# Five edits to a tuned hard-max attention kernel: the last four tiles compared whole, the first segment's rows as words, larger loads, gathers two a tile, key units later

## The chip, the cores and the metric

The kernel runs on one core of a Trainium2 chip. The metric is the device time of one execution in microseconds (us), as the median of the fast executions of a kernel. The kernel before takes 438.6 us. Every run of another kernel was made on one chip together with runs of the kernel before. A ratio is the mean time of one kernel's fast runs over that of the other's of the same rounds, so it is not quite the ratio of the medians that I quote; an interval is a 95% interval.

PE is TensorE, DVE is VectorE, ACT is ScalarE, POOL is GpSimd and SP is SyncE. A profile was taken of one execution of each kernel. All times within an execution are microseconds from the start of its span; "L310" is a line of the kernel that the profile is of, and line numbers differ a little from kernel to kernel.

## The reference

```python
# q, k, v: (4, 4096, 128) fp32, normal draws
logits = np.matmul(q, k.transpose(0, 2, 1))
best = np.argmax(logits, axis=-1)
return v[b_idx, best, :].astype(np.float32)
```

For each of 4 x 4096 queries the key with the greatest product is sought, and its row of v is the result. That is 128 tiles of 128 queries.

## The kernel before

For each tile, PE makes products in fp16 (`pd`, `psn`), ACT turns them into codes (`A`, `E`), and DVE folds them into words (`W`) and takes the eight greatest (`TOP`, a MAX8). The low bits of the best word name a group of keys (`cand`). POOL gathers those keys in fp16 (`kg`), DVE multiplies them with the queries (`prod`, `p1`, `p2`, `D`) and picks, and POOL gathers the rows of v (`vr`), which SP stores. Rows where fp16 can't decide are "flagged": their indices are compacted with one-hot matrices on PE, at tile 64 for the first half (a "segment") and after the last tile for the second, their keys and queries are gathered in fp32 (`FK`, `FQ`), compared, and their rows of v (`FV`) scattered over what was stored (`out`). Two more tiles, the last ones, are compared whole in fp32 (`gather_whole`, `dots_whole`, `pick_whole`), so that their candidates need no flags.

POOL issues all gathers and many loads, in the order in which this function hands them out once per tile:

```python
def issue(it):
    n = 0
    ...
    while near_q and (n < 1 + behind or near_q[0] in marks or it >= T - 1):   # kg: one a tile
        g = near_q.pop(0)
        n += g not in marks
        g()
    ...                                                                       # then vr, at a rate
```

```python
def gathers(t):
    ...
        m = 4 if t1 <= 116 else 2
        if t0 <= t < t1 and t < T - 2 and (t - t0) % m == m - 1:
            gather(c, t - m + 1, m)      # four kg come due at once
```

The loads of the next batches' keys and queries go out on the same POOL queue in 8-row pieces:

```python
        elif 10 <= qt < 18 and qt % 2 == 0:
            load_part(b + 1, qt - 2)
        elif 18 <= qt < 26 and qt % 2 == 0:
            load_part(b + 2, qt - 18)
```

The end of the program, after the last TOP, is: flags of the second segment up to the word index `row`, gathers of FK and FQ, exact comparison, FV, and then

```python
        get(FV, v_flat, win, B * Sk)
        nc.gpsimd.indirect_dma_start(out=out_flat, out_offset=IOA(ap=rowk, axis=0), in_=FV, ...)   # "out"
```

after which every engine runs its closing instructions.

## Time and profile before

| what | before |
|---|---|
| median time | 438.6 us |
| span of the profiled execution | 436.54 us |
| first TOP / last TOP (tile 127) start | 19.4 / 408.28 us |
| last TOP to the issue of `out` | 24.07 us |
| issue of `out` to the end of the span | 4.19 us |

The last three rows add up to the span (408.28 + 24.07 + 4.19): the loop, the tail, the end. How ACT, DVE and POOL share these stages is read in the prediction below. The view of groups: line, engine, operation, out <- in, shapes, count | busy us, mean ns of one | idle time of the engine before them, and what ended it.

```profile
L311 DVE TENSOR_TENSOR prod<-kg,natq 128x768 f16<-128x768 f16 x63 | 34.4, 546 | 0.2 <-DMA kg<-k,cand 0.2
...
L927 POOLq DRAIN  x3: 46/109/3253, 432.1 to 436.3; - x3
```

DVE waits 0.2 us in all for gathered keys. POOL's sequencer has three DRAINs in the closing code, the longest of 3.253 us, starting at 432.1, with the issue of `out`.

### The profile page before, as it was taken

To read this page: it belongs to the slowest core of one execution; us is meant where nothing else is said; L and a number is where in the kernel's file an instruction comes from. 1 tells how busy PE (TensorE), PEld (TensorE's weight loads), DVE (VectorE), ACT (ScalarE), POOL (GpSimd) and SP (SyncE) were. 2 spreads that over 40 slices of the span, in tenths; PEclk is the share of its full clock that TensorE was granted. 3 is DMA by queue.
4 is the path that set the end of the run, shared out by engine and by line. 5 is a ranking of instruction groups with operands and counts; after the bars stand their busy time and mean duration, and the time that the engine had idled before them with its cause. 6 is when DMAs were issued, how large, how long until landed. Compare 5 with 4: busy or idle time off the path is not lost.

```text
span 436.5 us, 6165 instructions
## 1 busy us (share of the span) xinstructions
PE 377.1 (86%) x1830; PEld 167.7 (38%) x1830; DVE 406.6 (93%) x722; ACT 378.2 (87%) x446; POOL 304.3 (70%) x335
## 2 busy tenths in 40 slices
PE   7999999999999999999999888989889988885010
PEld 4444444444444444444444433433333333332000
DVE  2788999999999999999999999999999999999961
ACT  4999999999999999999999888999999988985010
POOL 8423456777767786777778776777767677777773
PEclk9999999999999999999999999999999999999555
DMA  7943999473326999663336985452423232333441
GB/s 127 204 108 72 158 141 144 103 134 81 108 55 133 174 166 189 127 113 100 92 95 138 172 148 116 93 143 76 119 76 92 82 85 81 93 95 99 116 131 52
DMA packets 52868, 50.54 MB, mean 116 GB/s; under 512 B 34136, under 2 KB 40890, under 8 KB 52832
## 3 DMA queue, kind: packets, MB, share of 16 engines
q0 software_dynamic: 19072, 33.87, 39.7%
q1 hardware_dynamic: 33760, 16.26, 15.8%
q8 instruction: 14, 0.23, 0.2%
q14 instruction: 22, 0.18, 0.2%
HBM read 40.05 MB, written 14.55 MB: 125 GB/s over the span
## 4 chain that ended last, share of the span: by engine, by line
ACT 37%; issue 23%; DVE 16%; PE 9%; POOL 8%; DMA 6%; POOLq 0%; ACTq 0%; DVEq 0%; SPq 0%
ACT A L245 32%; DVE TOP L275 6%; ACT E L258 5%; DVE W L271 5%; POOL vr L353 4%; PE psn L228 3%; POOL kg L293 3%; PE pd L228 3%; PE psn L255 3%; DMA vr<-in_v_dram,win 2%; DMA natk<-in_k_dram 2%; DVE prod L311 1%; DVE p L316 1%; DMA vr<-in_v_dram,win_w 1%; DMA kg<-k,cand 1%
## 5 line engine op out<-in xcount | busy, mean ns | idle before, releaser
L245 ACT ACTIVATE A<-pd 128x1024 f16<-128x1024 f32 x253 | 257.0, 1043 | 10.8 <-PE pd L228 10.3
L293 POOL DMA_INDIRECT kg<-k,cand x126 | 124.5, 988 | 79.8 <-DVE cand L287 48.8
L271 DVE SCALAR_TENSOR_TENSOR W<-psn,E 128x1024 int16<-128x1024 f32 x128 | 166.4, 1300 | 6.8 <-PE psn L255 4.1
L228 PE MATMUL psn<-kT,qT 128*128 128x512 f16 x512 | 151.9, 378 | 16.2 <-ACT A L245 7.5
L228 PE MATMUL pd<-kT,qT 128*128 128x512 f16 x506 | 150.4, 379 | 6.6 <-ACT A L245 6.3
L275 DVE MAX8 TOP<-W 128x8 f32<-128x1024 f32 x128 | 156.0, 1219 | 0.0
L228 PEld LDWEIGHTS <-qT 128*128 128x128 f16 x1018 | 97.2, 97 | 153.0 <-issue 62.9
L353 POOL DMA_INDIRECT vr<-in_v_dram,win x126 | 125.9, 1000 | 39.5 <-issue 35.3
L255 PE MATMUL psn<-A,identh 128*128 128x512 f16 x512 | 152.0, 378 | 0.0
L258 ACT ACTIVATE E<-psn 128x1024 int16<-128x1024 f32 x128 | 132.3, 1033 | 4.6 <-PE psn L255 4.1
L255 PEld LDWEIGHTS <-identh 128*128 128x128 f16 x512 | 49.6, 97 | 60.8
L311 DVE TENSOR_TENSOR prod<-kg,natq 128x768 f16<-128x768 f16 x63 | 34.4, 546 | 0.2 <-DMA kg<-k,cand 0.2
L208 ACT ACTIVATE kT<-uk 128x256 f16<-128x256 f32 x48 | 20.4, 426 | 0.8 <-PE uk L205 0.8
L316 DVE TENSOR_TENSOR p<-prod 128x768 f16<-128x768 f16 (+1 forms) x34 | 17.7, 520 | 0.2
L321 DVE TENSOR_REDUCE D<-p 128x12 f32<-128x384 f16 (+1 forms) x34 | 17.2, 506 | 0.1
L204 PE MATMUL uk<-identh,natk 128*128 128x128 f16 x96 | 15.8, 218 | 0.0
L512 ACT ACTIVATE far_e<-iota_h,posn_e 128x128 f16<-128x128 f16 x2 | 0.8, 393 | 14.7 <-DVE posn_e L504 14.7
L495 PE MATMUL fp_e<-n_e,tri 128*128 128x1 f32 x2 | 0.6, 348 | 13.9 <-DVE n_e L493 13.9
L205 PEld LDWEIGHTS <-natk 128*128 128x128 f16 x96 | 9.3, 97 | 7.0 <-issue 4.5
L66 POOL DMA_DIRECT2D natk<-in_k_dram x19 | 11.3, 601 | 0.8 <-POOLq L916 0.8
L204 PEld LDWEIGHTS <-natk 128*128 128x128 f16 x96 | 9.4, 98 | 5.6
L319 DVE TENSOR_TENSOR p<-p 128x384 f16<-128x384 f16 (+1 forms) x34 | 11.3, 331 | 0.1
(158 smaller groups left out, 153.4 us busy)
## 6 DMA issues: line engine op xcount, KB each, us to landing
out_dram<-vr SPq DMA_DIRECT2D x31, 256.0 KB, 2.2
natq<-in_q_dram POOLq DMA_DIRECT2D x12, 256.0 KB, 5.3
natk<-in_k_dram POOLq DMA_DIRECT2D x10, 256.0 KB, 5.7
k<-kd SPq DMA_DIRECT2D x18, 128.0 KB, 3.4
k<-natk POOLq DMA_DIRECT2D x6, 384.0 KB
kg<-k,cand POOLq DMA_INDIRECT x126, 2.7
vr<-in_v_dram,win POOLq DMA_INDIRECT x126, 2.7
natk<-in_k_dram POOLq DMA_DIRECT2D x8, 128.0 KB, 6.5
```

What stands on the lines that cost most here:

```text
L204: nc.tensor.matmul(out=o, lhsT=natk[b % 2][:, h, 4 * m + x, :], rhs=identh, start=True, stop=False)
L208: nc.scalar.activation(out=kT[b % 2][:, c:c + 256], in_=ps, func=AF.Copy)
L228: nc.tensor.matmul(out=ps[:, n * 512:(n + 1) * 512], lhsT=qT[b % 2][:, qt * P:(qt + 1) * P], rhs=kT[b % 2][:, u * 1024 + n * 512:u * 1024 ...
L245: nc.scalar.activation(out=A, in_=ps, func=AF.Abs)
L255: nc.tensor.matmul(out=ps[:, n * 512:(n + 1) * 512], lhsT=identh, rhs=A[:, n * 512:(n + 1) * 512], start=False, stop=True)
L258: nc.scalar.activation(out=E, in_=ps, func=AF.Relu, scale=QSCALE)
L271: nc.vector.scalar_tensor_tensor(out=W_t[t % NW].bitcast(I16)[:, 1::2], in0=ps, scalar=QSCALE, in1=E, op0=OP.mult, op1=OP.max)
L275: nc.vector.max(out=TOP[:, t, :], in_=W_t[t % NW].bitcast(FP32))
L293: near_q.append(lambda j=j: nc.gpsimd.indirect_dma_start(out=kg[:, j].rearrange("p f d -> p (f d)"), out_offset=None, in_=k16[t0 // NQT], ...
L311: nc.vector.tensor_tensor(out=prod[:, i:i + h], in0=kg[:, i:i + h], in1=natq[b % 2][:, x + i - b * NQT:x + i + h - b * NQT, :].unsqueeze(2 ...
L316: nc.vector.tensor_tensor(out=p1, in0=prod[:, :, :, 0:64], in1=prod[:, :, :, 64:128], op=OP.add)
L353: late_q.append(lambda j=j: nc.gpsimd.indirect_dma_start(out=vr[:, j, :], out_offset=None, in_=v_flat, in_offset=IOA(ap=win[:, i + j:i + j ...
```

## The change

Its intent: (a) "whole": the last four tiles instead of two are compared whole in fp32, so their dots leave the tail; (b) "words": the first segment gets its keys' indices from words that are already there, as the second one does, rather than by fetching a record back; (c) "loads": 8-row pieces become 16-row pieces, at fewer tiles; (d) "gathers": two kg a tile instead of one from tile 4 to 111, so that dots start earlier; (e) "units": ACT's key units of the first batch three tiles later. Cut to its core:

```diff
-LATE = 4
+LATE = 2
+WHOLE = 4
...                                       # (b) in flag_segment, many small steps out, wider ones in
+        low_words(t0, S)
+        EC = ...tensor_tensor(CG * F)     # 4 x S at once, then four MAX8
-        nc.vector.tensor_copy(out=bs, in_=ps[:, 0:1])
+        nc.scalar.activation(out=bs, in_=ps[:, 0:1], func=AF.Copy)
-        get(FR, rec, rr, P * T)
+        gb, row = places(t0, ps2)
...                                       # (a)
-    cuts = list(range(0, 96 + 1, 8)) + list(range(96 + 4, T - 3, 4)) + [T - 2, T]
+    cuts = list(range(0, 96 + 1, 8)) + list(range(96 + 4, T - 7, 4)) + [T - 6, T - 4, T]
...                                       # (d)
-        while near_q and (n < 1 + behind or near_q[0] in marks or it >= T - 1):
+        while near_q and (n < (2 if 4 <= it < 112 else 1) + behind or near_q[0] in marks or it >= T - 1):
...                                       # (e)
-        units += [(x - 1, x - NQT + (6 + 3 * i // 2 if b == 1 else 1 + 2 * i), unit_k, b, i) for i in range(16)]
+        units += [(x - 1, x - NQT + (9 + 3 * i // 2 if b == 1 else 1 + 2 * i), unit_k, b, i) for i in range(16)]
...                                       # (c)
-        elif 10 <= qt < 18 and qt % 2 == 0:
-            load_part(b + 1, qt - 2)
-        elif 18 <= qt < 26 and qt % 2 == 0:
-            load_part(b + 2, qt - 18)
+        elif qt in (11, 19):
+            load_part(b + 1, 8 + (qt - 11) // 2, 16)
+        elif qt in (23, 27):
+            load_part(b + 2, qt - 23, 16)
```

## The prediction

> **What bounds the kernel now.** I read the page first (DVE busy 93%, ACT 87%, PE 86%, POOL 70% of 436.5 us), then the busy time by stretches, because a share averaged over the span hides stages with different limits. Columns: busy microseconds of PE, PEld, DVE, ACT and POOL in the stretch, then clock, DMA share, GB/s.
>
> ```profile
> 20.00:40.00 20.00, 19.13 (x98) 8.73 (x96) 16.77 (x17) 20.00 (x25) 5.24 (x6) 1.00 0.50 97
> 100.00:120.00 20.00, 19.64 (x96) 8.73 (x95) 20.00 (x31) 20.00 (x25) 14.23 (x16) 1.00 0.33 90
> ...
> 240.00:260.00 20.00, 17.50 (x91) 7.95 (x90) 19.94 (x45) 17.12 (x21) 15.47 (x17) 1.00 0.98 156
> ...
> 340.00:360.00 20.00, 17.81 (x76) 7.17 (x74) 19.83 (x31) 18.16 (x20) 14.15 (x15) 1.00 0.31 88
> ...
> 410.00:420.00 10.00, 1.36 (x8) 1.02 (x8) 8.19 (x52) 1.31 (x4) 7.61 (x8) 0.50 0.46 132
> 420.00:437.00 17.00, 0.59 (x2) 0.50 (x2) 5.24 (x40) 0.00 (x0) 7.96 (x8) 0.50 0.32 91
> ```
>
> There are three stages. Until about 240 us ACT is full, and DVE is full too from 60 us on; only before that has DVE slack (3.2 us in 20 to 40). From 240 us to about 409 us DVE alone is full and ACT waits. After the last TOP (408.28 us) comes a tail of 28 us with no large work. Next the groups, for the size of the steps, and the timeline, for what they really cost from start to start:
>
> ```profile
> L245 ACT ACTIVATE A<-pd 128x1024 f16<-128x1024 f32 x253 | 257.0, 1043 | 10.8 <-PE pd L228 10.3
> L293 POOL DMA_INDIRECT kg<-k,cand x126 | 124.5, 988 | 79.8 <-DVE cand L287 48.8
> L271 DVE SCALAR_TENSOR_TENSOR W<-psn,E 128x1024 int16<-128x1024 f32 x128 | 166.4, 1300 | 6.8 <-PE psn L255 4.1
> ```
>
> ```profile
> 102.51 1.22 DVE L275 MAX8 TOP<-W 128x8 f32<-128x1024 f32 x1
> 103.65 1.29 DVE L271 SCALAR_TENSOR_TENSOR W<-psn,E 128x1024 int16<-128x1024 f32 x1
> 104.82 0.55 DVE L311 TENSOR_TENSOR prod<-kg,natq 128x768 f16<-128x768 f16 x1
> 105.29 1.22 DVE L275 MAX8 TOP<-W 128x8 f32<-128x1024 f32 x1
> ```
>
> Start to start TOP takes 1.14, W 1.17 and prod 0.47 us: durations overlap, so a removed step gives back somewhat less than its duration. A tile needs W + TOP (2.31 to 2.34), a quarter of a four-tile dot group (two prod, 0.46, 0.26, 0.45: about 0.54) and a share of a pick: about 2.95 us on DVE, the pace until 208 us (TOP 0 to TOP 64: 188.6 us / 64). From there to TOP 127 it is 200.3 / 63 = 3.18 us, because the first segment's flags and the smaller picks are added on DVE.
>
> The tail, in order of time (start, duration):
>
> ```profile
> 408.28 1.23 DVE L275 MAX8 TOP<-W 128x8 f32<-128x1024 f32 x1
> ...
> 410.20 0.55 DVE L311 TENSOR_TENSOR prod<-kg,natq 128x768 f16<-128x768 f16 x1
> ...
> 411.94 0.95 POOL L580 DMA_INDIRECT xk<-in_k_dram,xc  x1 [0.30 <-DVE D L321]
> ...
> 413.19 1.10 POOL L353 DMA_INDIRECT vr<-in_v_dram,win  x1 [0.30 <-issue]
> ...
> 417.18 0.15 DVE L525 TENSOR_SCALAR row_e<-rs_e 128x1 uint32<-128x1 f32 x1
> ...
> 418.51 1.01 POOL L528 DMA_INDIRECT FK<-in_k_dram,gb_e  x1 [0.30 <-DVE XD L585]
> ...
> 426.44 1.02 POOL L353 DMA_INDIRECT vr<-in_v_dram,win_w  x1 [0.30 <-issue]
> 428.30 1.00 POOL L528 DMA_INDIRECT FV<-in_v_dram,xw_fe  x1 [0.84 <-DVE xw_fe L623]
> 432.35 1.02 POOL L557 DMA_INDIRECT out_dram<-FV,rowk_e  x1 [3.05 <-DMA out_dram<-vr]
> ```
>
> What is to be seen: POOL issues one gather every 1.3 us without a pause from 401 to 427 us (0.30 us between two that waits for nothing). The word index row_e is there at 417.33 us, yet FK starts 1.2 us later, behind four vr gathers. The last step waits for the store of the last vr pair (issued 426.44, landed 2.75 later, stored 2.09 later). So two chains run side by side in the tail, DVE to row_e and POOL's queue, and the queue is the later one.
>
> **What the Trainium skill says.** "Perfetto Trace Analysis", section "DMA Instruction — SWDGE (GPSIMD)": the profiled end of such a DMA is the end of descriptor generation, not of the data's movement. The trace agrees: a gather shows 0.95 to 1.0 us on POOL and lands 2.7 us after its issue (median in the DMA list), so a load twice as large need not cost POOL twice. "DMA: Bandwidth & Descriptors", section "Anatomy of one DMA — SWDGE (gpsimd) path": about 2.0 us fixed plus the bytes; the 2.7 us and the 5.3 to 5.7 us of the 256 KB loads fit in order. "VectorE: DVE Perf Modes", section "The TRN2 errata — SBUF-src ops pay a fixed extra latency per instruction": a small operation is mostly a fixed cost. Here operations on 1 to 12 elements take 0.13 to 0.23 us, so what counts in the flag code is their number. "ScalarE: Activation LUTs", section "What ACT_TABLE_LOAD costs": 186 ns + 0.833 ns per element, 93 ns overlap; for 1024 that is 1039 ns, and the trace has 1043.
>
> **The change part by part.**
>
> *Last four tiles whole.* The dots of tiles 124 and 125 leave the tail: from prod at 410.20 to the pick at 411.86, 1.66 us off DVE's chain to row_e. Picks keep their number (the last groups become 120-122 and 122-124, both done before TOP 127). One one-hot moves from ACT to DVE: DVE ends its four at 416.0, ACT its two at 416.64; with five and one both end near 416.1, 0.5 us less. Together row_e comes 2.2 us earlier, some 415.1. Eight further fp32 dot products at 0.21 us (417.29 to 419.00 for the present eight) add 1.7 us of DVE, but while FK and FQ are still coming. POOL gains nothing in count: 126 kg + 126 vr + 2 + 2 become 124 + 124 + 4 + 4, always 256 gathers. From 401.2 us to FV I count 20 of them before; written out in the new order (one xk, three vr, xk, two vr, xk, vr, xk, two vr, four FK/FQ, four vr of the whole tiles) it is 20 again. At 1.3 us each FK would start near 416.8, the last vr pair near 426.1 instead of 426.44 us. So of DVE's 2.2 us POOL lets through 0.3 to 1.6 us, the larger value if one vr that now runs at 398.49 is done before. Taken: 0.9.
>
> *First segment as words.* Removed on DVE, by the groups' durations: Ec 0.22, two sums 0.40, bs and tot 0.28, a cast 0.17, tp to row (seven) 1.01, rr twice 0.29, bo, gi, gb 0.50: 2.87 us. Added, from their twins in the last segment: CG 0.50, EC 0.43, three MAX8 0.47, two rec 0.35, gb, rs, row 0.46: 2.21 us. Net 0.66 us less, on a full DVE (240 to 320 us): taken as 0.5. ACT gets five small operations (an estimate of 1.5 us) in a stretch where it has 14% idle. POOL loses one gather (1.3 us) and a wait for it.
>
> *Loads.* 34 direct loads become 24 (8-row pairs merged); ten at 0.60 + 0.30 us free 9 us of POOL, but POOL sets nothing before the tail, and prod waits for kg only 0.2 us in the whole run. Value 0 directly.
>
> *Gathers two a tile.* The four kg of a group go out in two tiles rather than four, so its dots begin up to two tiles earlier. The number of operations stays. Its worth is at the start: two tiles' dots (2 x 0.54 us) move into DVE's slack before 60 us, out of the time in which DVE is full. Taken 0.6.
>
> *Key units three tiles later.* 16 of 48 ACT operations of 0.43 us move inside a stretch in which ACT is full before and after: 0.
>
> Sum: 0.9 + 0.5 + 0.6 = 2.0 us; 438.6 - 2.0 = 436.6, and I put 436.4 because a lighter POOL may start the tail less behind.
>
> **The rivals.** (1) *POOL's queue does not hold the tail*: if lighter loads leave POOL idle before 400 us, the whole 2.2 us of DVE, and the last pair with it, come through, and with DVE's gains in the loop the time is near 434. For it: POOL is 2 us behind DVE at xk (409.6 to 411.94), which ten fewer loads could remove. Against it: by then the vr of a pick start only about 3 us after it (win at 398.06, its first vr at 401.20), so the backlog of loads long past is already gone. (2) *The larger loads delay the kg behind them*, and DVE, which has no slack after 60 us, stands still: some 1 us for each of ten loads, 440 or more. For it: landings rise to 4 to 6 us beside loads. Against it: loads now go out at tiles 11, 19, 23, 27 of 32, and kg always at the two tiles before and again two tiles later, 5.9 us apart. (3) *Nothing but noise*: four vr of the whole tiles instead of two come after FK and end later than now, eating the gain: 438.5. (4) The ACT copies of bs and tot stand in ACT's queue, and posn waits there: up to 1 us worse.
>
> **Range and chances.** The parts spread from -5 to +2 us; 8 in 10 from 433.8 to 438.9. Faster by 2% would need 429.8 us, more than every gain I can name together; slower by 2% (447.4) would need rival 2 at four times its size.
>
> **What would show it.** The steps hold if TOP 127 starts 0.5 to 1.5 us earlier, if the stretch 20 to 60 us has more DVE work, if the way from TOP 127's start to row_e's end (408.28 to 417.33, 9.05 us) shrinks by about 2 us, and if POOL is still without pauses until the last vr pair. A wait of prod for kg above 1 us in total would make rival 2 right. POOL with pauses before FK would make rival 1 right. A TOP 127 that starts later than 408.3 would make the prediction wrong in the loop, where I expect almost nothing.

## The result, and the profile after

The changed kernel takes 443.68 us (443.13 to 443.88, 4 runs) against 438.53: ratio 1.0114, interval [1.0096, 1.0131]. It is 1.1% slower where 0.5% faster was predicted.

| | before | after | difference |
|---|---|---|---|
| last TOP | 408.28 | 411.28 | +3.00 |
| last TOP to `out` | 24.07 | 23.23 | -0.84 |
| `out` to the end of the span | 4.19 | 7.34 | +3.15 |
| span | 436.54 | 441.85 | +5.31 |

So the tail did what was predicted (0.9 us), and two losses stand against it: one in the loop, one after the last transfer was issued. The stretches first (PE, PEld, DVE, ACT, POOL busy; clock; DMA share; GB/s), of the changed kernel:

```profile
20.00:40.00 20.00, 19.44 (x93) 8.57 (x92) 17.82 (x18) 20.00 (x25) 5.23 (x6) 1.00 0.56 101
...
240.00:260.00 20.00, 17.90 (x94) 8.31 (x94) 19.90 (x42) 18.37 (x29) 13.71 (x14) 1.00 0.79 143
280.00:300.00 20.00, 17.78 (x87) 7.79 (x86) 19.03 (x44) 18.22 (x23) 13.47 (x14) 1.00 0.47 111
```

DVE has 1.05 us more work in 20 to 40 (17.82 against 16.77), as the prediction wanted. ACT is full in that stretch, and nothing comes of it: TOP of tile 20 starts 0.10 us earlier than before, TOP of tile 32 starts 0.2 us later. Between 280 and 300 us, where DVE was full before (19.97 us), it stands still for a microsecond. The groups of the changed kernel say what for:

```profile
L292 POOL DMA_INDIRECT kg<-k,cand x124 | 121.0, 976 | 90.2 <-DVE cand L286 59.5
...
L310 DVE TENSOR_TENSOR prod<-kg,natq 128x768 f16<-128x768 f16 x62 | 34.1, 550 | 2.8 <-DMA kg<-k,cand 2.8
```

The wait of prod for kg has grown from 0.2 to 2.8 us. POOL is less busy than before (67% against 70%), so it isn't overloaded on average. The timeline (start, duration, engine, line, operation, idle time before it) shows how the wait comes about, here for the first one:

```profile
145.14 0.95 POOL L352 DMA_INDIRECT vr<-in_v_dram,win  x1 [0.30 <-issue]
146.40 1.39 POOL L352 DMA_INDIRECT vr<-in_v_dram,win  x1 [0.30 <-issue]
147.79 1.36 POOL L97 DMA_DIRECT2D k<-natk  x1
149.45 1.45 POOL L292 DMA_INDIRECT kg<-k,cand  x1 [0.30 <-issue]
151.20 0.98 POOL L292 DMA_INDIRECT kg<-k,cand  x1 [0.30 <-issue]
152.49 0.95 POOL L292 DMA_INDIRECT kg<-k,cand  x1 [0.30 <-issue]
153.74 0.94 POOL L292 DMA_INDIRECT kg<-k,cand  x1 [0.30 <-issue]
...
156.01 0.56 DVE L310 TENSOR_TENSOR prod<-kg,natq 128x768 f16<-128x768 f16 x1 [0.59 <-DMA kg<-k,cand]
```

Four kg in a row, 149.45 to 154.68, with vr gathers and a transfer to k ahead of them. A prod multiplies two tiles, so the one at 156.01 needs the first two kg. By the records of their semaphores, the second of these, issued at 151.20, landed at 155.91: 4.7 us later, not the 2.8 us that the list of issues gives as the median, and after DVE had begun to wait. In the kernel before the same four (tiles 40 to 43) were issued from 148.39 to 156.06, and their first prod started at 160.75. Over the groups of tiles 12 to 107 the time from the issue of the second kg to that prod is 5.5 us in the median in the changed kernel and 9.2 before. Landings as slow as that are not new: between 130 and 200 us, where the loads are under way, half of the 23 kg of the kernel before whose landing the trace records took more than 4.1 us, and the slowest 7.5. Before, the program left them the time; now it doesn't.

The tail and the closing line of the changed kernel:

```profile
411.28 1.23 DVE L274 MAX8 TOP<-W 128x8 f32<-128x1024 f32 x1
417.29 0.15 DVE L386 TENSOR_SCALAR row<-rs 128x1 uint32<-128x1 f32 x1
419.72 1.00 POOL L504 DMA_INDIRECT FK<-in_k_dram,gb  x1 [0.30 <-DVE XD L561]
428.92 1.00 POOL L352 DMA_INDIRECT vr<-in_v_dram,win_w  x1 [0.30 <-issue]
434.51 1.03 POOL L533 DMA_INDIRECT out_dram<-FV,rowk_e  x1 [3.28 <-issue]
```

```profile
L904 POOLq DRAIN  x3: 46/109/6740, 434.3 to 441.6; - x3
```

From the start of the last TOP to the end of row it is now 6.16 us instead of 9.05, but FK starts only 1.79 us earlier after TOP than before (8.44 against 10.23), and `out` 0.84 us: POOL's queue holds the rest back. Then the closing DRAIN lasts 6.74 us instead of 3.25. It starts with the issue of `out` in both kernels (0.23 us before it), so it doesn't start late, and it isn't waiting for the data of `out`: in all twenty kernels of this document the last packet of POOL's queue ends 0.84 us after that issue has ended and the last semaphore update of `out` comes 1.17 to 1.28 us after it, while the DRAIN ends 2.00 us after it before and 5.48 us in the changed kernel.

### The profile page after: what moved, and what is told of

Same layout as the page of the kernel before. It is cut to its first block, busy times and chain, and to the rows that moved or that the text cites. A ratio compares the mean times of both kernels' runs of the same rounds, so it can differ in the third digit from the quotient of the medians.

```text
span 441.9 us, 6156 instructions
## 1 busy us (share of the span) xinstructions
PE 380.0 (86%) x1832; PEld 168.6 (38%) x1832; DVE 408.3 (92%) x727; ACT 379.1 (86%) x451; POOL 297.2 (67%) x323
## 4 chain that ended last, share of the span: by engine, by line
DVE 26%; issue 19%; PE 18%; ACT 16%; POOL 10%; DMA 8%; POOLq 0%; ACTq 0%; DVEq 0%; SPq 0%
ACT A L244 13%; DVE TOP L274 10%; DVE W L270 8%; PE pd L227 6%; PE psn L227 6%; POOL vr L352 6%; PE psn L254 5%; DMA kg<-k,cand 4%; POOL kg L292 3%; ACT E L257 3%; DVE prod L310 2%; DMA natk<-in_k_dram 2%; DMA FK<-in_k_dram,gb 2%; DVE p L315 1%; DVE D L320 1%
## 5 line engine op out<-in xcount | busy, mean ns | idle before, releaser
L292 POOL DMA_INDIRECT kg<-k,cand x124 | 121.0, 976 | 90.2 <-DVE cand L286 59.5
L66 POOL DMA_DIRECT2D natk<-in_k_dram x15 | 8.7, 590 | 0.8 <-POOLq L893 0.8
```

Source lines behind the costliest of these rows:

```text
L292: near_q.append(lambda j=j: nc.gpsimd.indirect_dma_start(out=kg[:, j].rearrange("p f d -> p (f d)"), out_offset=None, in_=k16[t0 // NQT], ...
```

## The experiments

My theory for the loop (B) was that two gathers a tile bring kg late. Its rival was the prediction's own rival 2, that the larger loads delay the kg behind them. For the end, the first theory (A, later P) was that the length of POOL's program decides the DRAIN, since the trace shows instructions being fetched by DMA as the program runs (22 packets of 8 KB in queue q14). In the tables, "TOP" is the start of the last TOP, "tail" from there to `out`, "end" from `out` to the end of the span; "kg" is prod's wait for kg. All runs were correct.

### 1. A longer program for POOL: e1_pad18, e5_pad40, e7_beforeless

```diff
 # e1: the changed kernel, e5 the same with 40
+        if it == 2:
+            for _ in range(18):
+                nc.gpsimd.memset(padt, 0.0)
 # e7: the kernel before
-    nc.gpsimd.memset(ones, 1.0)      # and six others
+    nc.vector.memset(ones, 1.0)
```

Expected of e1_pad18:

> The changed kernel with 18 one-element memsets on GpSimd at tile 2, where it idles; they bring its instruction count back to the old kernel's (488 in the trace of before, 470 after). Theory A: the closing DRAIN of GpSimd (6.74 us in the changed kernel, 3.25 us before) depends on where its instruction stream ends, so here it returns to about 3.3 us and the time falls by 3 to 3.5 us, to about 440.3. Rival: the drain waits for the traffic of the four whole tiles or for something else in the tail, so it stays at 6.7 us and the time at 443.7.

Expected of e5_pad40:

> The changed kernel with 40 one-element GpSimd memsets at the third tile, so GpSimd's program is 892 instructions long instead of 852 (the kernel before: 871, short closing DRAIN; 852, 854 and 868 had the long one, 867 had one of each). Theory P (where the end of GpSimd's program falls in its instruction pages decides the closing DRAIN): at 892 the DRAIN is short as in the kernel before, about 3.2 us instead of 6.7, and the run takes about 440.2 us. Theory Q (it doesn't depend on the length of the program): DRAIN 6.7 us and 443.7 us. The loop is expected as in the first padded run in both (last TOP 411, wait for kg 2 to 2.8 us).

Expected of e7_beforeless:

> The kernel before with its seven clearing memsets of the start on VectorE instead of GpSimd; GpSimd's program is 863 instructions instead of 871. Theory P: shorter than 867, so the closing DRAIN is long, 6.7 us, and the kernel takes about 442 us though nothing in its loop has changed. Theory Q: DRAIN 3.2 us and 438.5 us. The last TOP stays within 0.4 us of 408.3 in both.

| | median | ratio, interval | TOP | kg | tail | end | longest DRAIN |
|---|---|---|---|---|---|---|---|
| e1_pad18 | 443.66 | 1.0119 [1.0100, 1.0137] | 410.88 | 2.02 | 23.17 | 7.34 | 6.73 |
| e5_pad40 | 443.86 | 1.0127 [1.0107, 1.0147] | 410.76 | 2.21 | 23.67 | 7.34 | 6.74 |
| e7_beforeless | 438.99 | 1.0005 [0.9988, 1.0021] | 408.67 | 0.00 | 24.41 | 4.18 | 3.26 |

The DRAIN did not move by more than 0.02 us in any of the three. The number of POOL's instructions is not its cause, and theory A and P fall. (Counted in the traces, POOL has 480 instructions in e7, 485 in e4 and 488 in the kernel before, all with the short one, and 485 in e3, 486 in e1 and 508 in e5, with the long one.)

### 2. Gathers and loads undone in the changed kernel: e2_noG, e3_noL, e4_noGL

```diff
 # e2, e4: gathers one a tile again
-        while near_q and (n < (2 if 4 <= it < 112 else 1) + behind or ...
+        while near_q and (n < 1 + behind or ...
 # e3, e4: loads in 8-row pieces at the old tiles (as in the diff of the change, reversed)
```

Expected of e2_noG:

> The changed kernel with the candidate gathers back to one a tile. Theory B: the loop's 3.0 us come from prod waiting for kg (2.8 us in the changed kernel, 0.2 before), because four gathers in two tiles crowd GpSimd's queue; here that wait falls below 0.6 us and the last TOP starts at 408.3 to 409.3 us instead of 411.3. Rival (loads): the wait stays above 2 us. Rival (first segment as words): the last TOP stays near 411. The end drain may go either way.

Expected of e3_noL:

> The changed kernel with the loads back to 8-row pieces at the old tiles. Rival to theory B: the 16-row loads hold up the gathers behind them; then prod's wait for kg falls below 0.6 us and the last TOP starts near 408.5. Theory B: the gathers still come in pairs and now meet more loads, so the wait stays at 2 us or more and the last TOP at 411 or later. GpSimd's stream is ten DMAs longer than the changed kernel's: theory A allows another end drain.

Expected of e4_noGL:

> Both undone: gathers one a tile, loads in 8-row pieces at the old tiles. What is left of the change is the last tiles whole, the first segment as words and the later key units. Theory B: wait for kg about 0.2 us, last TOP at 407.5 to 409; if the word form of the first segment costs DVE time, it shows here as a last TOP later than 409.

| | median | ratio, interval | TOP | kg | tail | end |
|---|---|---|---|---|---|---|
| after | 443.68 | 1.0114 [1.0096, 1.0131] | 411.28 | 2.79 | 23.23 | 7.34 |
| e2_noG | 442.2 | 1.0081 [1.0064, 1.0099] | 409.31 | 0.68 | 24.49 | 7.32 |
| e3_noL | 448.44 | 1.0222 [1.0205, 1.0240] | 415.79 | 6.10 | 23.39 | 7.99 |
| e4_noGL | 440.66 | 1.0039 [1.0017, 1.0061] | 409.01 | 0.91 | 25.63 | 4.29 |

Theory B holds: without the second gather the wait for kg falls by 2.1 us and the last TOP comes 2.0 us earlier. (Two forecasts were missed: the wait is 0.68 us in e2, not under 0.6, and 0.91 in e4, not 0.2.) That the two figures agree is partly chance. Against e2, DVE's idle time between the first and the last TOP is only 1.05 us greater in the changed kernel (6.82 against 5.77), because it is 0.9 us smaller up to tile 32, where the prediction wanted it smaller; the other 0.98 us is time in which DVE's instructions, 609 in both, run longer or overlap less. The trace doesn't say why. The rival falls, and in the other direction than expected: with the *old, smaller* loads the two gathers cost more, not less.

```profile
L310 DVE TENSOR_TENSOR prod<-kg,natq 128x768 f16<-128x768 f16 x62 | 34.0, 548 | 6.1 <-DMA kg<-k,cand 6.1
```

That line is of e3. So the larger loads are what makes the two gathers bearable; between 130 and 200 us the kg landed after 4.0 us in the median in e3 and after 3.3 in the changed kernel. And the end became short, 4.29 us, only when both were undone; e3 and e4 have the same instructions and the same transfers on POOL, in another order.

### 3. One part alone in the kernel before: e11_before_L, e12_before_G

The edits are (c) alone and (d) alone, as in the diff of the change.

Expected of e11_before_L:

> The kernel before with the loads in 16-row pieces alone. The prediction gave the loads nothing. If the long closing DRAIN comes with the loads whatever else is changed, it is 6.7 us here, the last TOP stays within 0.4 us of 408.3, and the time is 442 us; if it needs another part of the change as well, it is 3.2 us and the time 438.6 us.

Expected of e12_before_G:

> The kernel before with two candidate gathers a tile alone. Theory B (two gathers a tile bring kg late, and the small loads make that worse): VectorE's products wait for kg 4 to 7 us and the last TOP is 3.5 to 7 us later than 408.3, as in the run of the change with the old loads (6.1 us, last TOP 415.8); rival: with the other parts of the change gone the two gathers cost under 1 us. If the long closing DRAIN comes with the gathers too, it is 6.7 to 7.4 us here, and the time 446 to 450 us; if not, 442 to 446 us.

| | median | ratio, interval | TOP | kg | tail | end | longest DRAIN |
|---|---|---|---|---|---|---|---|
| e11_before_L | 442.27 | 1.0085 [1.0068, 1.0102] | 408.75 | 0.42 | 23.63 | 7.39 | 6.78 |
| e12_before_G | 452.4 | 1.0332 [1.0300, 1.0365] | 417.09 | 6.65 | 24.86 | 8.07 | 7.46 |

Larger loads alone leave loop and tail as they were within half a microsecond each and still cost 3.7 us, nearly all of it in the closing DRAIN. Two gathers a tile alone cost 13.8 us in the median: 8.8 in the loop, 0.8 in the tail and 3.9 at the end by the profile; up to 7 us in the loop were expected. Its timeline shows the small loads inside the bursts:

```profile
164.98 0.98 POOL L293 DMA_INDIRECT kg<-k,cand  x1 [0.30 <-issue]
165.94 0.65 POOL L66 DMA_DIRECT2D natk<-in_k_dram  x1
166.89 0.99 POOL L293 DMA_INDIRECT kg<-k,cand  x1 [0.30 <-issue]
168.18 0.95 POOL L293 DMA_INDIRECT kg<-k,cand  x1 [0.30 <-issue]
...
170.26 0.56 DVE L311 TENSOR_TENSOR prod<-kg,natq 128x768 f16<-128x768 f16 x1 [1.31 <-DMA kg<-k,cand]
```

A load of 8 rows comes at every second tile and so falls between the kg of a burst, at 0.9 us a piece; 16-row loads come at other tiles and half as often. From the first kg of a group to the fourth it takes 4.5 us in the median here and in e3, 3.9 in the changed kernel. But this is not the whole of it: the two kg that the prod at 170.26 needs were issued at 163.63 and 164.98, before the load shown, and landed after 5.7 and 5.2 us. How much of the wait is late issue and how much slow landing was not separated.

### 4. The other parts one after the other: e6_whole, e8_wholewords

```diff
 # e6: the changed kernel with (b), (c), (d) and (e) undone: whole last tiles alone
 # e8: with (c), (d) and (e) undone: whole last tiles and words
```

Expected of e6_whole:

> The kernel before with the last four tiles compared whole and nothing else of the change: loads, gathers, key units and first segment as before. If the whole tiles do what the prediction's sum gave them, the time from the last TOP to the scatter of out is 0.8 us shorter than before (24.07 us) and the last TOP stays at 408.3; with a short closing DRAIN that is 437.7 us, with a long one 441.2. Rival: the 0.7 us by which the last TOP was late without the gathers and the loads comes from the whole tiles (their later checks and picks at the end of the loop); then the last TOP is at 409.0.

Expected of e8_wholewords:

> Whole last tiles and first segment as words, with loads, gathers and key units as before. Against the run with whole tiles alone it shows the words by themselves, against the earlier run without the gathers and the loads it shows the later key units by themselves. Prediction of record: words are worth 0.5 us less in the loop, key units nothing: last TOP 0.5 us earlier than with whole tiles alone and 409.0 or earlier. Rival: the words are what made the last TOP 0.7 us late (their copies on ScalarE, which is full until 240 us, and the segment's later steps between 208 and 250 us): last TOP at 409.0 here and at 408.3 with the whole tiles alone.

With these the change can be put together part by part:

| kernel | median | TOP | tail | end | span |
|---|---|---|---|---|---|
| before | 438.6 | 408.28 | 24.07 | 4.19 | 436.54 |
| + whole (e6) | 438.63 | 408.82 | 23.50 | 4.21 | 436.53 |
| + words (e8) | 441.45 | 409.55 | 25.86 | 4.30 | 439.71 |
| + units (e4) | 440.66 | 409.01 | 25.63 | 4.29 | 438.93 |
| + loads (e2) | 442.2 | 409.31 | 24.49 | 7.32 | 441.12 |
| + gathers (after) | 443.68 | 411.28 | 23.23 | 7.34 | 441.85 |

(Ratios of e6 0.9999 [0.9983, 1.0016], of e8 1.0062 [1.0045, 1.0078].) Each row is one profile. Six kernels that differ by padding or tiny loads alone (the changed one, e1, e5, e13, e14, e16) have their last TOP between 410.69 and 411.55 and their tails between 23.17 and 25.57 us, so loop differences of half a microsecond are not clear of noise, and a part's share also depends on what was already in. Whole tiles alone come out even: 0.57 us won in the tail, 0.54 lost in the loop, of which 0.24 is there at the first TOP already. Words cost 2.8 us, 0.7 of it in the loop and 2.4 in the tail, which they don't touch by their own code. Units win 0.8 us by the medians, but e8 and e4 ran in different calls and their intervals overlap, so this is not shown.

For the words in the loop I added up the time in which DVE has an instruction running between the first TOP and the last: 383.4 us without them (e6), 383.7 with them (e8). The 2.87 us that were to be removed and the 2.21 to be added thus leave 0.2 more, not 0.66 less. The traces show why, if each instruction is counted only until the next one starts: the removed ones then take 1.56 us (2.91 by durations), because most of the small ones overlap by half, and the added ones 1.60 (2.34), because CG and EC, 0.50 and 0.40 us long, keep 0.42 and 0.33. Of the 0.73 us by which the last TOP is later, the rest is idle time; prod waits for kg 0.65 us in e8 and not at all in e6. For the words in the tail the records of transfers give a reading that I did not test: in e8 the last vr pair is stored 13.27 us after the first FK instead of 12.21, and just before that a fetch of instructions (8 KB, 5.59 to 5.28 us before `out`) is followed at its very end, at 5.28, by one lone packet of 4 bytes of POOL's queue. The same pair is there in e2, e4, e10, e13 and e14, and in these six that store is issued 12.90 to 13.27 us after the first FK; in the seven others with four whole tiles, which have no such pair, at 11.95 to 12.36. It looks as if the end of a gather stood behind the fetch. Another 1.3 us between that store and `out` have no cause that I can name; e4 and e13 have them as well, the two other kernels with 308 transfers and a short DRAIN (part 7), which was not followed up. Both are gone again in the changed kernel (tail 23.23), so they are no part of its 5.3 us.

### 5. More transfers on POOL's queue: e9_after_dummy, e10_whole_dummy

```diff
+        if it in (1, 2, 3, 4):
+            for _ in range(3):           # e10: whole tiles alone, with 2
+                nc.gpsimd.indirect_dma_start(out=zv, out_offset=None, in_=v_flat, in_offset=IOA(ap=zi, axis=0))
```

Expected of e9_after_dummy:

> The changed kernel with twelve gathers more, three at each of tiles 1 to 4, into a tile that nobody reads, on the same GpSimd queue. Theory R (the long closing DRAIN is work that GpSimd does on its queue of software descriptors at the end, and its length follows from what was queued before): the DRAIN changes from 6.7 us, to some 3.2 or to another length. Theory T (it comes from something that these gathers don't touch): it stays at 6.7 us within 0.1. The loop is the same or a little later at the start; the last TOP 411 to 412 us.

Expected of e10_whole_dummy:

> Whole last tiles alone (closing DRAIN 3.25 us, 438.6 us) with eight gathers more, two at each of tiles 1 to 4, into a tile that nobody reads. Theory R: the DRAIN can get long, 6.7 us or another length, and the run 442 us. Theory T: 3.25 us and 438.6 to 439.2 us.

The times are spoilt by a mistake of mine: all these gathers write one tile, and each waits for the one before to land, which held POOL up at the start.

```profile
  POOL zv L812: 32.4, 11
```

That line, from the view of the tile zv of e9, says that POOL waited 32.4 us at 11 of them. So e9 takes 471.23 us (ratio 1.0745 [1.0727, 1.0763], last TOP 440.81) and e10 449.1 (1.0234 [1.0217, 1.0251], 418.80), and their medians say nothing of the change. Their ends do:

```profile
L910 POOLq DRAIN  x3: 46/109/3177, 463.3 to 467.4; - x3
```

With twelve transfers more the changed kernel has the *short* DRAIN, 3.177 us. In e10 it is 3.580. So the DRAIN follows from what has been queued before (theory R), although it comes hundreds of microseconds later. The hold-up at the start is a rival here; the next part takes it away.

### 6. How many transfers: e13_after_tiny10, e14_after_tiny20, e15_beforeL_tiny10, e16_after_tiny5

```diff
+        if 1 <= it <= 10:                # each into a tile of its own: nothing waits
+            nc.gpsimd.dma_start(out=zv.pop(), in_=v[0][0:P, 0:1])
```

That is e13, and e15 on top of e11; e14 has two at each of these tiles, e16 one at each of tiles 1 to 5.

Expected of e13_after_tiny10:

> The changed kernel with ten more direct loads on GpSimd's queue, one at each of tiles 1 to 10, of 4 bytes a partition into tiles that nobody reads, so that the queue carries 308 transfers as the runs with the short closing DRAIN did (308 to 316) and not 298. Theory N (the number of transfers that were queued before sets the closing DRAIN when the rest is the same): DRAIN 3.2 us, end 440.2 us. Theory O (only their order or the gathers do): DRAIN 6.7 us, 443.7 us. The last TOP stays at 411 to 412 us.

Expected of e14_after_tiny20:

> As the run with ten more loads, with twenty (318 transfers). Theory N: DRAIN short, 3.2 to 3.6 us (316 transfers gave 3.58), unless the length comes round again. Theory O: 6.7 us.

Expected of e15_beforeL_tiny10:

> The kernel before with the loads in 16-row pieces, and ten tiny direct loads that nobody reads to bring GpSimd's queue back to 309 transfers. With the loads alone the DRAIN was 6.78 us and the time 442.3. Theory N: DRAIN 3.2 us and 438.9 us. Theory O: 6.8 us and 442.3 us. Last TOP within 0.5 us of 408.8 in both.

Expected of e16_after_tiny5:

> As the run with ten more loads, with five (303 transfers). It shows where between 298 and 308 the DRAIN changes and whether it has lengths between 3.2 and 6.7 us. Theory N with a step: either of the two; theory N with a slope: about 5 us. Theory O: 6.7 us.

(The count of 316 in the first text was one off; the trace of e10 has 317.) One run of the kernel before took 996 us and was left out as slow.

| | transfers | median | ratio, interval | TOP | tail | end | longest DRAIN |
|---|---|---|---|---|---|---|---|
| e16_after_tiny5 | 303 | 443.63 | 1.0104 [1.0086, 1.0122] | 411.55 | 23.40 | 7.80 | 7.18 |
| e13_after_tiny10 | 308 | 442.25 | 1.0067 [1.0047, 1.0087] | 410.69 | 25.57 | 4.29 | 3.14 |
| e14_after_tiny20 | 318 | 441.52 | 1.0066 [1.0044, 1.0089] | 411.24 | 24.27 | 4.12 | 3.46 |
| e15_beforeL_tiny10 | 309 | 442.6 | 1.0084 [1.0066, 1.0102] | 408.50 | 24.28 | 8.12 | 7.50 |

Adding twenty loads that nobody needs made the changed kernel 2.2 us *faster* in the median, because the end is 3.2 us shorter. With ten the DRAIN is short as well, but the time is 442.25 and not 440.2, because the tail is 2.3 us longer (part 4). But e15 fell out against theory N: 309 transfers as in the kernel before, and the longest end of all so far. Neither the count alone nor the order alone decides between long and short. Within the long ones, though, the end grows with the count, and that led to the last theory.

### 7. The kernel before with more transfers: e17_before_tiny30, e18_before_tiny60

The edit is that of part 6 in the kernel before, at tiles 1 to 30 and 1 to 60.

Expected of e17_before_tiny30:

> The kernel before, otherwise untouched, with thirty tiny loads that nobody reads on GpSimd's queue, one at each of tiles 1 to 30 (339 transfers instead of 309). In the runs so far the closing DRAIN ended 5.48 us after the last issue at 298 transfers, 5.52 at 299, 5.92 at 303, 6.13 to 6.25 at 308 and 309 (0.067 us for each transfer more), or else 1.9 to 2.3 us at 308 to 318, 4.2 us less, which is as much as 63 transfers. Theory N2 (the DRAIN works through the transfers left since the queue was last cleared, and the queue is cleared in steps of about 64): with 30 more it ends 2.0 + 30 x 0.067 = 4.0 us after the last issue instead of 2.0, or, if a clearing falls in between, under 2.0. Theory O (order and timing, not the count): 2.0 us.

Expected of e18_before_tiny60:

> As the run with thirty, with sixty, one at each of tiles 1 to 60 (369 transfers). Theory N2: 2.0 + 60 x 0.067 = 6.0 us, or 4.2 to 4.3 us less, 1.7 to 1.8, if it has been cleared once more; theory O: 2.0 us.

This chip was a disturbed one: the kernel before took 522.68 us on it (509.34 to 532.84), e17 530.71 and e18 535.69, with granted clocks of 0.89 to 0.93; I use no time of these runs. The DRAIN runs after all the work, and its own length is what was asked:

```profile
L931 POOLq DRAIN  x3: 46/109/5143, 527.4 to 533.1; - x3
```

```profile
L931 POOLq DRAIN  x3: 46/109/7582, 519.0 to 527.1; - x3
```

Counted from the end of the last issue it ends 3.88 us later in e17 (expected 4.0) and 6.33 in e18 (expected 6.0), where the kernel before has 2.00. The rival that the count doesn't matter falls. All runs together, ordered by the transfers on POOL's queue (gathers and direct loads):

| transfers | DRAIN's end after the last issue's end, us |
|---|---|
| 298 (after, e1, e2, e5) | 5.47 to 5.48 |
| 299 (e11), 303 (e16) | 5.52, 5.92 |
| 308 (e3), 309 (e12, e15) | 6.13, 6.21, 6.25 |
| 308 (e13, e4, e8) | 1.88, 1.96, 1.96 |
| 309 (before, e6, e7) | 2.00 |
| 310 (e9), 317 (e10), 318 (e14) | 1.92, 2.33, 2.21 |
| 339 (e17), 369 (e18) | 3.88, 6.33 |

There are two rows of values. From 298 to 309 the upper one rises by (6.21 - 5.48) / 11 = 0.067 us a transfer; from the kernel before to e17 the lower one by (3.88 - 2.00) / 30 = 0.063, and from e17 to e18 by 0.082. Pairs of one kernel spread more: 0.033 from e13 to e14, 0.041 from e6 to e10, 0.073 from e11 to e15, 0.088 from the changed kernel to e16. Packets don't order the rows as well: e15 and e12 have 17952 and 19072 on this queue and end at 6.25 and 6.21. At 308 and 309 the two rows lie 4.2 us apart, the worth of some 63 transfers. So the DRAIN behaves as if POOL worked through a list of the transfers queued since it last cleared the list, with clearings some 64 transfers apart, and the changed kernel ended just before one and the kernel before just after one. That it grows with the count is measured, the slope only roughly. The list and its clearing are only a reading that fits; no record shows them, and what decides whether the last clearing falls before the end (e3 against e4, the same transfers in another order) stays open.

No run beats the kernel before. Whole tiles alone equal it, and nothing in the table of parts except perhaps the units won time; the kernel before with the later units alone was not run.

## Why the prediction was wrong

The predicted time was 436.4 us in a range up to 438.9, and 443.68 was measured; the class (within 2%) was right. By its own steps:

- *Last four tiles whole, 0.9 us.* Right in mechanism and nearly in size. Row comes 2.9 us earlier after TOP (2.2 predicted), POOL's queue lets part of it through, and the tail is 0.84 us shorter in the changed kernel. Measured alone it is 0.57 us, and the loop takes 0.54 back, which was not in the sum.
- *First segment as words, 0.5 us.* Wrong. The step that failed is "Removed ... 2.87 us. Added ... 2.21 us". The prediction had itself read from the timeline that durations overlap, and then summed durations of 0.13 to 0.22 us as if they didn't. Counted from start to start, 1.56 us went and 1.60 came. DVE is covered 0.2 us longer with the words, and the last TOP is 0.7 us later, a figure within the spread of single profiles.
- *Loads, 0.* Wrong by 3.0 us: their value for POOL before the tail is indeed nothing (last TOP +0.3), but with them the closing DRAIN went from 3.2 to 6.7 us. Rival 2, which feared them for the kg, was wrong about them too: prod did wait over 1 us for kg, the very sign that I had named for it, and undoing the loads raised the wait to 6.1 us.
- *Gathers two a tile, 0.6 us.* Wrong in sign: 2.0 us lost in the loop. The dots did move into DVE's slack (0.9 us less idle up to tile 32 than in e2), but TOP of tile 32 comes no earlier; ACT is full there, as the prediction's own table says. The step that failed is the wait: "so its dots begin up to two tiles earlier" looks only at when four kg can be issued, not at whether they have landed. From the issue of the second kg to its prod there are 5.5 us where there were 9.2, and between 130 and 200 us landings take 4 to 7 us. The prediction knew of those ("landings rise to 4 to 6 us beside loads") and charged them to the loads alone.
- *Key units, 0.* Perhaps 0.5 to 0.8 us better, which is not clear of noise: DVE's idle time up to tile 32 falls from 4.0 us (e8) to 3.4 (e4).
- *What the sum left out.* It ended with `out`. The 4.19 us after it were taken as fixed and became 7.34. This term alone, 3.15 us, is more than all gains that the prediction counted, and the greatest part of its miss. No run before the prediction showed that it can change. Without this term and the 2.0 us of the gathers the time would have been some 438.5 us, just inside the range.

Of the signs named, TOP 127 later than 408.3 came true and showed the loop wrong. POOL without pauses, a shorter way to row and more DVE work from 20 to 60 us came true as well. The reading of POOL's queue in the tail was good: FK was put at 416.8 us and the last vr at 426.1, and counted from the last TOP, as if it were at 408.28, they come at 416.72 and 425.92. One reading was too kind: that landings of 2.7 us and of 5.3 to 5.7 us "fit in order" a fixed cost plus the bytes says only that the larger take longer; the sum was not worked out, and between 130 and 200 us a kg, always of the same size, took up to 7.5 us.

## What to carry to other kernels

Issuing transfers earlier is not the same as having them earlier: when a queue is handed a burst, check for each part of the burst that its issue and its landing, at the speed that landings have in that stretch and not in the median of the run, fit into the time until the program uses it. Test a suspect by undoing it rather than by its symptom; here the wait for kg pointed at the loads, and the loads were what kept it small. And read a trace to its last instruction: a change in how transfers are queued at the start can come back microseconds long in the closing code.

## What the Trainium skill lacked or had wrong

- "VectorE: DVE Perf Modes", section "The DRAIN you can't avoid", tells of two DRAINs, the flush after a VectorE operation and that of the runtime's code around a kernel, "~12 ns constant" on all five engines. The one that cost time here is neither as described: the trace puts it on GpSimd, at the kernel's own closing line, and it lasted 3.14 to 7.58 us in twenty kernels, 3.5 us longer in the changed kernel than before. No page has it.
- "DMA: Bandwidth & Descriptors", section "Anatomy of one DMA — SWDGE (gpsimd) path", tells what one such transfer costs. It lacks what the transfers cost together at the end: 0.03 to 0.09 us of closing DRAIN for each transfer more on the queue, with drops of about 4.2 us in between.
- No page has a figure for what an instruction fetch costs a transfer on another queue. In six kernels here a lone last packet of GpSimd's queue came at the very end of a fetch of 0.3 us, and the store that waited for a gather was issued 12.90 to 13.27 us after the first FK instead of 11.95 to 12.36; that the fetch held the packet up was not tested.
